# Single PSUM banks, moved sums and a four-buffer weight ring in a hybrid decoder block

## The chip, the cores and the metric

The kernel runs on one core of a Trainium2 chip. The metric is device time in microseconds (us) of one execution, as the median of the runs shown. The engines are TensorE (PE in the profile, its weight loads PEld), VectorE (DVE), ScalarE (ACT), GpSimd (POOL) and SyncE (SP, which issues the DMAs here).

## What is computed

One decoder block over 512 tokens of 1024 channels, all in float32: a mixer (a Mamba-2 scan and a causal pooling, merged by gates), a residual, and an MLP. The change lies where the mixer ends and the MLP begins, and in how the accumulator banks are named everywhere.

```python
h = rmsnorm(x, norm_mix_w) * (1.0 + scale_m) + shift_m
x = x + gate_m * hybrid_mixer(h, w_in, conv_w, ..., w_branch_ssd, pool_w, ..., w_branch_pool, w_out)
h = rmsnorm(x, norm_mlp_w) * (1.0 + scale_f) + shift_f
x = x + gate_f * (jnp.square(jax.nn.relu(h @ w_up)) @ w_down)      # 1024 -> 4096 -> 1024
return rmsnorm(x, norm_final_w)
# shift_*, scale_*, gate_* = split(silu(c) @ w_ada + b_ada): 48 columns of 128
```

## The kernel before, in words

**Layout.** Channels lie on the 128 partitions and the 512 tokens (T) along the free axis; a weight unit gives 128 output channels. Every float32 operand is split into a rounded part `hi` and a rest `lo` (ACT makes `hi`, DVE makes `lo`), and a product is three matmuls, hi·hi, hi·lo and lo·hi (`mm3`, L158 to L162). A unit of 1024 by 128 weights is 8 × 3 = 24 matmuls of 512 columns.

**Order of the work.** The first part (L220 to L299) is an order written out by hand. Everything behind it is handed to a scheduler, which orders the instructions of each engine by their place in the program, with the ones under `tc.high_priority()` first. Within one buffer the users come in program order. An engine then executes its list strictly in order, and the waits between engines follow from who writes and reads which tile.

**Buffers.** `Slots` (L43) is a first-in first-out list of buffers: `get` takes the oldest free one. `RAW` holds weights as they arrive, 4 buffers until the MLP, then 8, of which the last four lie in two large `sz` tiles (L754 to L756). `HL` holds split weights (8, in the MLP 12). `S` has 50 tiles of 512 columns. The `pad` tiles are left over from the pooling; in the MLP `U` (pads 0 and 1) holds the output of an up unit while it is squared and split, `Y4` (pads 5 and 8) a quarter of a pair's weights.

**Accumulators.** PSUM has eight banks of 512 columns. Banks 0 to 3 are single tiles `ps0` to `ps3`. Banks 4 to 7 are the halves of two tiles of two banks, `duo0` (4 and 5) and `duo1` (6 and 7), allotted once (L94 to L100). `PU` serves the weight units, `PS` the scan; from the gates on (L648) `PU` has all eight. The profile calls the tiles `ps` and `duo`.

**The mixer.** Four groups of the scan (`ssd_group`, L419) are woven with the weight units of the next group. `sc`, the scores, keeps one bank of `PS` for the whole group and is read by DVE at L452; `bk` is copied out of a bank by ACT at L429; the transposes (L455) and the output `yd` (L499) take further banks. Then come 8 gate units, 8 pool units (L654 to L658, DVE reads each bank at L656), 8 more gate units and 8 units of `w_out`.

**The modulation.** `ada(j)` (L172) loads 512 KB of `w_ada` into a `RAW` buffer and reduces it on DVE to column j of `mod` (L176). Each call stands behind a unit; the last three (45 to 47) stand behind the two halves of the norm (L742).

**The turn to the MLP.** The last three units of `w_out` run by halves of the tokens (L726), each half followed by the norm (L733) and the modulated row `h2` (hi and lo) with its unsplit source `hf` (8 tiles: six `S`, two `U`). Then `run_jobs` (L869) goes through a list of jobs; before a job runs, the weights of the next one are loaded.

- `up_first` (L937): four up units at once, by halves, in banks `PU`, `PU`, `AC`, `AC` (the free list of `PU` is 2 and 3 from L817, that of `AC` 0 and 1). Behind its matmuls stand, in program order, the shift of `hf` on ACT (L945), the sums `h2t` of `hf` (L947: four DVE operations of 256 columns, two casts and two subtractions for each of four pairs, L768 to L775), one matmul into each `duo` tile (L952), and then `activated` (L919) for the four banks: Relu (L922) into a tile of `U`, Square (L923), cast and subtraction (L765, L766).
- four `up_plain` jobs (L961), one unit each, in a bank of `PU`.
- three times: eight `down_plain` units and four `Pair` jobs (Strassen-like products of 256 columns, two banks of `BE` and one of `AC`, L825 to L863), which need `h2t`. The Relu of a pair reads its two `BE` banks in one instruction of 2 × 256 columns.
- the last down units and the final norm.

Of the kernel before, what the change touches and what calls it, by code (L numbers as in the profile page):

```python
# [7 lines left out]
F32 = mybir.dt.float32  # L8
F32R = mybir.dt.float32r
AF = mybir.ActivationFunctionType  # L10
ALU = mybir.AluOpType

P = 128
T = 512
# [24 lines left out]
OTHER = (0, 1, 4, 5, 8)  # L39
H = T // 2  # L40
# [21 lines left out]
def block_kernel(tc, xT, crow, arow, par, adaT, wstart, wz, wx, wpool_in, wgate, wpw, wbs, wbp, wout, wup, wdn, out):  # L62
# [3 lines left out]
    with (  # L66
# [6 lines left out]
        def slots(name, n, shape=(P, T), where=sb, first=0):  # L73
            def make(i, dt):
                count[0] += 1
                i += first
                return where.tile(list(shape), dt, tag=f"{name}{i}", name=f"{name}{i}_{count[0]}", bufs=1)
            return Slots(make, n)
# [3 lines left out]
        def D(i, dt, o=0):  # L82

            count[0] += 1
            w = 1024 if i < NRAW else 1088
            return sb.tile([P, w], dt, tag=f"d{i}", name=f"d{i}_{count[0]}", bufs=1)[:, o:o + 1024]
# [3 lines left out]
        MT = Slots(lambda i, dt: D(NRAW + NHL + i, dt).rearrange("p (h k) -> p h k", h=HG), 3)  # L90
        SM = slots("sm", 4, (P, NC))
        SM.put(*[SM.get() for _ in range(4)])

        duo = [psp.tile([P, 2, T], F32, name=f"duo{i}") for i in range(2)]  # L94

        def bank(i, dt):
            if i >= 4:
                return duo[(i - 4) // 2][:, i % 2, :]
            count[0] += 1
            return psp.tile([P, T], F32, tag=f"ps{i}", name=f"ps{i}_{count[0]}", bufs=1)  # L100

        PU, PS = Slots(bank, 8), Slots(bank, 8)
        PU.free, PS.free = PU.free[:NPU], PS.free[NPU:]

        par_t = sb.tile([P, NPAR], F32, name="par_t")
# [66 lines left out]
        def ada(j, at=RAW):  # L172

            r = at.get()
            sp.dma_start(r, adaT[j])
            dve.tensor_tensor_reduce(r, r, cbc, 1.0, col("b_ada", j), ALU.mult, ALU.add, mod[:, j:j + 1])  # L176
            at.put(r)
# [536 lines left out]
        for j in range(5):  # L714
            ps = unit(wout[j], mg)
            residual(ps, j, 16)
            PU.put(ps)
            ada(40 + j)
        for k in range(8):
            dve.tensor_scalar(  # L720
                amod[:, 8 + k:9 + k], mod[:, 32 + k:33 + k], 1.0, col("nmlp", k), ALU.add, ALU.mult)
        w = [load_unit(wout[j], at=S, cols=T) for j in (5, 6, 7)]
        h2 = [(S.get(F32R), S.get(F32R)) for _ in range(8)]
        U = Slots(lambda i, dt: slots("pad", 1, (P, T + 16), first=OTHER[i]).get(dt)[:, :T], 2)
        hf = [S.get() for _ in range(6)] + [U.get() for _ in range(2)]
        for t0, t1 in HALVES:  # L726
            for j in (5, 6, 7):
                ps = PU.get()
# [10 lines left out]
                dve.scalar_tensor_tensor(lo, t, shift, hi.bitcast(F32), ALU.add, ALU.subtract)  # L739
            PU.put(R)  # L740
        free(mg)
        for j in range(45, 48):  # L742
            ada(j)

# [5 lines left out]
        for p_, t in zip((SZ, SZ), later):  # L752
            p_.put(t)
        raws = [SZ.get(), SZ.get()]  # L754
        RAW = Slots(lambda i, dt: D(i, dt) if i < 4 else
                    raws[i // 2 - 2][:, 2 * (i % 2):2 * (i % 2) + 2, :].rearrange("p a b -> p (a b)"), 8)  # L756
        HL = Slots(lambda i, dt: D(NRAW + i, dt, 48), 12)
        HL0 = Slots(lambda i, dt: D(NRAW + i, dt), 12)
        HL0.free = HL.free
        Y4 = Slots(lambda i, dt: slots("pad", 1, (P, T + 16), first=OTHER[3 + i]).get(dt)[:, :T], 2)  # L760
        Y4S = Slots(lambda i, dt: slots("pad", 1, (P, T + 16), first=APART[i][0]).get(dt)[:, APART[i][1]:APART[i][1] + T], 4)

        def two(src, dst):
# [13 lines left out]
        def moving(plain, ts):  # L777

            cut = lambda t, i: tuple(x[:, i * H:(i + 1) * H] for x in t)
            return {  # L780
                "B11": [cut(plain[2 * m], 0) for m in range(4)],
                "B21": [cut(plain[2 * m + 1], 0) for m in range(4)],
                "B22": [cut(plain[2 * m + 1], 1) for m in range(4)],
                "T1": [cut(ts[m][0], 0) for m in range(4)], "T3": [cut(ts[m][0], 1) for m in range(4)],
                "T4": [cut(ts[m][1], 0) for m in range(4)], "T2": [cut(ts[m][1], 1) for m in range(4)],
            }
# [25 lines left out]
            Y4.put(y4)  # L812
            return {"S1": s1, "A11": a11, "S2": s2, "A12": a12, "S4": s4, "S3": s3, "A22": a22}

        BE = Slots(lambda i, dt: duo[i][:, :, :], 2)
        AC = slots("ps", 2, (P, T), psp)
        PU.free = [2, 3]  # L817

# [6 lines left out]
        class Pair:  # L825
            def __init__(self, w, b, done):
                self.w, self.b, self.done = w, b, done
# [3 lines left out]

            def open(self):
                self.be, self.s5 = BE.get(), U5.get()
                self.c11, self.c12 = self.be[:, 0, :H], self.be[:, 1, :H]
                product(self.c12, self.a["S1"], self.b["T1"], True)
                with tc.high_priority():
                    act.copy(self.s5, self.c12)
# [18 lines left out]

            def close(self):
                product(self.c12, self.a["S4"], self.b["B22"])
                self.done(0, self.be[:, :, :H], 1)
                BE.put(self.be)  # L860
                product(self.ac[:, :H], self.a["A22"], self.b["T4"])
                self.done(1, self.ac.rearrange("p (a b) -> p a b", a=2), -1)
                AC.put(self.ac)  # L863

        s5_t = slots("pad", 1, (P, T + 16), first=OTHER[2]).get()[:, :T]
        U5 = Slots(lambda i, dt: s5_t[:, i * H:(i + 1) * H], 2)
        ab = lambda t: t.rearrange("p (a b) -> p a b", a=2)

        def run_jobs(jobs):  # L869

            last = None
            jobs[0].prepare()
            for n, job in enumerate(jobs):
                after = jobs[n + 1] if n + 1 < len(jobs) else None
                if isinstance(job, Pair):
                    if n == 0 or not isinstance(jobs[n - 1], Pair):
                        job.open()
                    job.first()
                    if last:
                        last.close()  # L880
                    if after:
                        after.prepare()
                    job.middle()
                    if isinstance(after, Pair):
                        after.open()
                    job.third()
                    last = job
                else:
                    if last:
                        last.close()  # L890
                    last = None
                    if after:
                        after.prepare()
                    job.run()

        def load_plain(src, i, at=None, cols=1024):

# [14 lines left out]
            RAW.put(r)  # L912
            return [parts[4 * (k % 2) + k // 2] for k in range(8)]

        h2t = [[(S.get(F32R), S.get(F32R)) for _ in range(2)] for _ in range(4)]
        us = []
        hb = moving(h2, h2t)

        def activated(q, p, i, ps, sign):  # L919

            u = U.get()
            act.activation(ab(u), ps, AF.Relu, scale=float(sign))  # L922
            act.activation(u, u, AF.Square)  # L923
            two(u, us[2 * p + i])
            U.put(u)

        class Plain:
            def __init__(self, load, run):
                self.load, self.body = load, run

# [5 lines left out]

        def up_first(w):  # L937

            ps = [PU.get(), PU.get(), AC.get(), AC.get()]
            for t0, t1 in HALVES:  # L940
                for k in range(8):
                    for i in range(4):
                        mm3(ps[i][:, t0:t1], w[i][k], h2[k], k == 0, k == 7, t0, t1)
            for k in range(8):
                act.activation(hf[k], hf[k], AF.Identity, bias=mod[:, 24 + k:25 + k])  # L945
            for m in range(4):
                sums(*hf[2 * m:2 * m + 2], *h2t[m])  # L947
            S.put(*hf[:6])
            U.put(*hf[6:])
            us.extend((S.get(F32R), S.get(F32R)) for _ in range(8))  # L950
            for b in duo:
                pe.matmul(b[:, 0, :], h2[0][0][:, :P], h2[0][0], start=True, stop=True)  # L952
            for i in range(4):
                activated(0, i // 2, i % 2, ab(ps[i]), 1)
            PU.put(*ps[:2])
            AC.put(*ps[2:])

        def up(q, p):
            return Pair(wup[4 * q + p], hb, lambda i, ps, sign: activated(q, p, i, ps, sign))

        def up_plain(p, i):  # L961

            def f(w):
                ps = PU.get()
                for k in range(8):
                    mm3(ps, w[k], h2[k], k == 0, k == 7)
                activated(0, p, i, ab(ps), 1)
                PU.put(ps)
            return Plain(lambda: load_plain(wup[p], i), f)

# [49 lines left out]
                PU.put(R)  # L1020

        jobs = [Plain(lambda: [load_plain(wup[i // 2], i % 2, HL) for i in range(4)], up_first)] + [up_plain(p, i) for p in (2, 3) for i in range(2)]
        for q in range(3):
            jobs += [down_plain(q, (0, 1))] + [down_plain(q, (j,)) for j in range(2, 8)] + [up(q + 1, p) for p in range(4)]
        jobs += [down_plain(3, (0, 1))] + [down_plain(3, (j,)) for j in (2, 3, 4)]
# [80 lines left out]
```

## Time and profile before

| | |
|---|---|
| median of 3 runs | 1003.28 us (1002.08 to 1005.58) |
| the profiled execution | 1003.27 us |
| its span, first to last instruction | 1001.6 us |
| mean granted TensorE clock | 0.992 |
| busy in the span | PE 970.7, DVE 668.3, ACT 522.5, POOL 62.5 us |
| DMA | 129.62 MB, mean 129 GB/s |

1.67 us of the profiled execution lie outside its span. PE is busy for all but 30.9 us of it, so the table of waits, restricted to PE, is the shortest way to what could be saved: its rows say which instruction of PE stood idle, and the last event it had waited for. A row "PE ps L160 <- ACT pad L922: 6.8, 1, 6.8" reads: matmuls of line 160 into tiles `ps` waited for an ACT instruction of line 922, 6.8 us in total, in 1 wait, the longest of 6.8 us. In the timeline a row is start, duration, engine, line, operation, out<-in, shape, count, and in brackets the idle time just before. Matmuls overlap, so the rate of PE is the distance from start to start, not the duration.

### The profile page before, as it was taken

Reading aid. Unit: us, or ns where it says so; the run is one execution under the profiler, and the core shown is the slowest. Engines: PE = TensorE matmul, PEld = TensorE weight load, DVE = VectorE, ACT = ScalarE, POOL = GpSimd, SP = SyncE. Lnnn points to the kernel's source line nnn. Section 1 sums busy time; section 2 is a strip of 40 time slices with the busy share of each in tenths; the row PEclk is TensorE's granted clock in tenths of the full one; section 3 lists DMA queues with packets and bytes.
Section 4 is the critical chain, followed back from the end, with each engine's and each line's share of the span. In section 5 each row is a group of like instructions: output and inputs, shape, how many; then the busy total and the mean of one; then the engine's idle time right before and its main releaser. Section 6 shows DMA issues by size and latency. Waiting matters only on the chain.

```text
span 1001.6 us, 13351 instructions
## 1 busy us (share of the span) xinstructions
PE 970.7 (97%) x5174; PEld 815.4 (81%) x5174; DVE 668.3 (67%) x969; ACT 522.5 (52%) x805; POOL 62.5 (6%) x71
## 2 busy tenths in 40 slices
PE   8998999999999999999999999979999999999997
PEld 6877787887878878777878888968899889889986
DVE  6995959467766886888774565675557646755533
ACT  5497997677438733463312342574236326524732
POOL 0101220120102022200000000000000000000000
PEclk9999999999999999999999999989999999999998
DMA  9746343433353234437875444331224125213102
GB/s 349 288 129 190 104 130 105 108 125 101 100 147 106 85 100 121 137 125 251 274 244 167 155 158 130 102 98 53 64 96 158 53 74 170 70 56 132 38 1 84
DMA packets 62913, 129.62 MB, mean 129 GB/s; under 512 B 4801, under 2 KB 29505, under 8 KB 62850
## 3 DMA queue, kind: packets, MB, share of 16 engines
q1 hardware_dynamic: 62850, 128.77, 40.1%
q8 instruction: 40, 0.66, 0.3%
q14 instruction: 23, 0.19, 0.1%
HBM read 126.53 MB, written 2.23 MB: 129 GB/s over the span
## 4 chain that ended last, share of the span: by engine, by line
PE 57%; DVE 6%; DMA 5%; issue 4%; ACT 2%; POOL 1%; POOLq 0%; DVEq 0%; ACTq 0%
PE ps L160 12%; PE ps L161 12%; PE ps L162 12%; PE ps L823 7%; PE duo L823 5%; DMA d<-adaT 3%; PE duo L160 2%; PE duo L161 2%; PE duo L162 2%; DVE d L176 1%; POOL pad L567 1%; PE duo L499 1%; DVE d L766 0%; PE duo L483 0%; ACT d L150 0%
## 5 line engine op out<-in xcount | busy, mean ns | idle before, releaser
L160 PE MATMUL ps<-s,d 128*128 128x512 f32 (+1 forms) x930 | 360.8, 389 | 9.8 <-ACT pad L922 6.8
L161 PE MATMUL ps<-s,d 128*128 128x512 f32 (+1 forms) x930 | 354.9, 382 | 0.9 <-DVE s L131 0.8
L162 PE MATMUL ps<-s,d 128*128 128x512 f32 (+1 forms) x930 | 354.5, 381 | 0.0
L160 PEld LDWEIGHTS ps<-s,d 128*128 128x128 f32 x930 | 175.0, 188 | 48.9 <-ACT pad L922 7.5
L161 PEld LDWEIGHTS ps<-s,d 128*128 128x128 f32 x930 | 175.3, 188 | 35.4 <-issue 1.8
L162 PEld LDWEIGHTS ps<-s,d 128*128 128x128 f32 x930 | 175.0, 188 | 34.2 <-issue 0.6
L150 ACT CAST d<-d 128x1024 fp32r<-128x1024 f32 x89 | 92.8, 1044 | 111.7 <-PE ps L161 56.1
L151 DVE TENSOR_TENSOR d<-d,d 128x1024 fp32r<-128x1024 f32 x89 | 110.9, 1247 | 55.5 <-ACT d L150 50.5
L765 ACT CAST d<-d 128x1024 fp32r<-128x1024 f32 x40 | 41.7, 1049 | 86.1 <-PE ps L161 60.7
L765 ACT CAST d<-sz 128x1024 fp32r<-128x1024 f32 x36 | 37.6, 1050 | 74.3 <-PE ps L161 54.5
L994 DVE SCALAR_TENSOR_TENSOR xs<-ps,mod,xs 128x512 f32<-128x512 f32 x29 | 21.5, 751 | 69.3 <-PE ps L162 69.3
L766 DVE TENSOR_TENSOR d<-d,d 128x1024 fp32r<-128x1024 f32 x40 | 48.7, 1224 | 23.2 <-ACT d L765 21.5
L766 DVE TENSOR_TENSOR d<-sz,d 128x1024 fp32r<-128x1024 f32 x36 | 43.9, 1224 | 28.1 <-ACT d L765 25.1
L160 PE MATMUL duo<-s,d 128*128 128x512 f32 (+1 forms) x158 | 59.4, 378 | 2.8 <-DVE xs L656 2.4
L161 PE MATMUL duo<-s,d 128*128 128x512 f32 (+1 forms) x158 | 58.8, 372 | 0.0
L162 PE MATMUL duo<-s,d 128*128 128x512 f32 (+1 forms) x158 | 58.6, 372 | 0.0
L823 PE MATMUL duo<-s,d 128*128 128x256 f32 x432 | 58.1, 282 | 0.0
L823 PE MATMUL ps<-s,d 128*128 128x256 f32 x432 | 55.9, 280 | 0.1
L823 PEld LDWEIGHTS duo<-s,d 128*128 128x128 f32 x432 | 53.7, 188 | 2.6 <-DVE duo L848 1.5
L823 PEld LDWEIGHTS ps<-s,d 128*128 128x128 f32 x432 | 53.0, 188 | 0.7 <-ACT duo L843 0.7
L176 DVE CUSTOM_DVE_ANT_0 d<-d,d,par_t 128x1024 f32<-128x1024 f32 x32 | 40.8, 1278 | 16.9 <-DMA d<-adaT 16.7
L451 ACT ACTIVATE d<-d,ncs 128x128 f32<-128x128 f32 x128 | 41.3, 391 | 10.7 <-POOL d L447 10.5
(268 smaller groups left out, 1263.3 us busy)
## 6 DMA issues: line engine op xcount, KB each, us to landing
d<-adaT SPq DMA_DIRECT2D x32, 512.0 KB, 4.3
d<-wx SPq DMA_DIRECT2D x18, 512.0 KB, 3.6
d<-wz SPq DMA_DIRECT2D x16, 512.0 KB, 3.4
d<-cs_d SPq DMA_DIRECT2D x16, 512.0 KB, 5.8
d<-wbs SPq DMA_DIRECT2D x16, 512.0 KB, 3.4
d<-wgate SPq DMA_DIRECT2D x16, 512.0 KB, 3.9
d<-wdn SPq DMA_DIRECT2D x16, 512.0 KB, 3.9
sz<-wdn SPq DMA_DIRECT2D x16, 512.0 KB, 3.9
```

Of the source, the lines that this page charges most:

```text
L150: act.copy(hi[:, :w], r[:, a:a + w])
L151: (low or dve).tensor_tensor(lo[:, :w], r[:, a:a + w], hi[:, :w].bitcast(F32), ALU.subtract)
L160: pe.matmul(ps, whi, xhi[:, t0:t1], start=start, stop=False)
L161: pe.matmul(ps, whi, xlo[:, t0:t1], start=False, stop=False)
L162: pe.matmul(ps, wlo, xhi[:, t0:t1], start=False, stop=stop)
L176: dve.tensor_tensor_reduce(r, r, cbc, 1.0, col("b_ada", j), ALU.mult, ALU.add, mod[:, j:j + 1])
L451: act.activation(m[:, i, :], m[:, i, :], AF.Exp, bias=ncs[:, c, g * HG + i:g * HG + i + 1])
L499: pe.matmul(yd[o:o + 64, i * P:(i + 1) * P], xdt[:, i * P + o:i * P + o + 64], m[:, 2 * i + hh, :], start=True, stop=True)
L765: act.copy(dst[0], src)
L766: dve.tensor_tensor(dst[1], src, dst[0].bitcast(F32), ALU.subtract)
L823: pe.matmul(ps, x, y, start=start and m == 0 and i == 0, stop=m == 3 and i == 2, skip_group_check=True)
L994: dve.scalar_tensor_tensor(x1[j], ps[i], mod[:, 40 + j:41 + j], x1[j], ALU.mult, ALU.add)
```

## The change

All eight banks become single tiles `ps0` to `ps7`; the two `BE` banks of a pair are two of them, and the Relu of a pair's first output is two instructions of 256 columns. `up_first` takes the two `AC` banks and the second banks of the two `BE` pairs in place of `PU`'s, so `PU`'s two banks stay free for the plain units. `hf`'s last two tiles are `Y4`'s in place of `U`'s. The shift and the sums of `hf` become a function that stands behind the fourth plain up unit. `RAW` has four buffers until then and eight from there on. `ada(45)` to `ada(47)` stand behind the units 2, 3 and 4 of `w_out`.

```diff
-        duo = [psp.tile([P, 2, T], F32, name=f"duo{i}") for i in range(2)]
-        def bank(i, dt):
-            if i >= 4:
-                return duo[(i - 4) // 2][:, i % 2, :]
...
-        PU, PS = Slots(bank, 8), Slots(bank, 8)
+        PU, PS = slots("ps", 8, (P, T), psp), slots("ps", 8, (P, T), psp)
...
             ada(40 + j)
+            if j > 1:
+                ada(43 + j)
...
-        U = Slots(lambda i, dt: slots("pad", 1, (P, T + 16), first=OTHER[i]).get(dt)[:, :T], 2)
-        hf = [S.get() for _ in range(6)] + [U.get() for _ in range(2)]
+        Y4 = Slots(lambda i, dt: slots("pad", 1, (P, T + 16), first=OTHER[3 + i]).get(dt)[:, :T], 2)
+        hf = [S.get() for _ in range(6)] + [Y4.get() for _ in range(2)]
...
-        for j in range(45, 48):
-            ada(j)
...
+        RAW.free = RAW.free[:4]
...
-        BE = Slots(lambda i, dt: duo[i][:, :, :], 2)
+        banks = [slots("ps", 1, (P, T), psp, first=4 + i).get() for i in range(4)]
+        BE = Slots(lambda i, dt: (banks[2 * i], banks[2 * i + 1]), 2)
...
-                self.done(0, self.be[:, :, :H], 1)
+                self.done(0, (self.c11, self.c12), 1)
...
                     job.run()
+                    if job.after:
+                        job.after()
...
-            act.activation(ab(u), ps, AF.Relu, scale=float(sign))
+            n = T // len(ps)
+            for i_, part in enumerate(ps):
+                act.activation(u[:, n * i_:n * (i_ + 1)], part, AF.Relu, scale=float(sign))
...
         def up_first(w):
-            ps = [PU.get(), PU.get(), AC.get(), AC.get()]
+            ps = [AC.get(), AC.get(), banks[1], banks[3]]
...
-            for k in range(8):
-                act.activation(hf[k], hf[k], AF.Identity, bias=mod[:, 24 + k:25 + k])
-            for m in range(4):
-                sums(*hf[2 * m:2 * m + 2], *h2t[m])
-            S.put(*hf[:6])
-            U.put(*hf[6:])
             us.extend((S.get(F32R), S.get(F32R)) for _ in range(8))
-            for b in duo:
-                pe.matmul(b[:, 0, :], h2[0][0][:, :P], h2[0][0], start=True, stop=True)
+            for b in banks[::2]:
+                pe.matmul(b, h2[0][0][:, :P], h2[0][0], start=True, stop=True)
...
+        def h2_sums():
+            for m in range(4):
+                for k in (2 * m, 2 * m + 1):
+                    act.activation(hf[k], hf[k], AF.Identity, bias=mod[:, 24 + k:25 + k])
+                h2t.append([(S.get(F32R), S.get(F32R)) for _ in range(2)])
+                sums(*hf[2 * m:2 * m + 2], *h2t[m])
+                if m < 3:
+                    S.put(*hf[2 * m:2 * m + 2])
+            Y4.put(*hf[6:])
+            RAW.free += range(4, 8)
+            hb.update(moving(h2, h2t))
...
+        jobs[-1].after = h2_sums      # jobs: up_first and the four up_plain
```

More of the change, by code (lines that the diff above doesn't have):

```diff
@@ L92, in block_kernel @@
         SM.put(*[SM.get() for _ in range(4)])
-        duo = [psp.tile([P, 2, T], F32, name=f"duo{i}") for i in range(2)]
-        def bank(i, dt):
-            if i >= 4:
-                return duo[(i - 4) // 2][:, i % 2, :]
-            count[0] += 1
-            return psp.tile([P, T], F32, tag=f"ps{i}", name=f"ps{i}_{count[0]}", bufs=1)
-        PU, PS = Slots(bank, 8), Slots(bank, 8)
+        PU, PS = slots("ps", 8, (P, T), psp), slots("ps", 8, (P, T), psp)
         PU.free, PS.free = PU.free[:NPU], PS.free[NPU:]
@@ L759, in block_kernel @@
         HL0.free = HL.free
-        Y4 = Slots(lambda i, dt: slots("pad", 1, (P, T + 16), first=OTHER[3 + i]).get(dt)[:, :T], 2)
+        U = Slots(lambda i, dt: slots("pad", 1, (P, T + 16), first=OTHER[i]).get(dt)[:, :T], 2)
         Y4S = Slots(lambda i, dt: slots("pad", 1, (P, T + 16), first=APART[i][0]).get(dt)[:, APART[i][1]:APART[i][1] + T], 4)
@@ L833, in open @@
                 self.be, self.s5 = BE.get(), U5.get()
-                self.c11, self.c12 = self.be[:, 0, :H], self.be[:, 1, :H]
+                self.c11, self.c12 = self.be[0][:, :H], self.be[1][:, :H]
                 product(self.c12, self.a["S1"], self.b["T1"], True)
@@ L858, in close @@
                 product(self.c12, self.a["S4"], self.b["B22"])
-                self.done(0, self.be[:, :, :H], 1)
+                self.done(0, (self.c11, self.c12), 1)
                 BE.put(self.be)
                 product(self.ac[:, :H], self.a["A22"], self.b["T4"])
-                self.done(1, self.ac.rearrange("p (a b) -> p a b", a=2), -1)
+                self.done(1, (self.ac,), -1)
                 AC.put(self.ac)
@@ L866, in block_kernel @@
         U5 = Slots(lambda i, dt: s5_t[:, i * H:(i + 1) * H], 2)
-        ab = lambda t: t.rearrange("p (a b) -> p a b", a=2)
         def run_jobs(jobs):
@@ L913, in load_plain @@
             return [parts[4 * (k % 2) + k // 2] for k in range(8)]
-        h2t = [[(S.get(F32R), S.get(F32R)) for _ in range(2)] for _ in range(4)]
-        us = []
-        hb = moving(h2, h2t)
+        us, h2t, hb = [], [], {}
         def activated(q, p, i, ps, sign):
             u = U.get()
-            act.activation(ab(u), ps, AF.Relu, scale=float(sign))
+            n = T // len(ps)
+            for i_, part in enumerate(ps):
+                act.activation(u[:, n * i_:n * (i_ + 1)], part, AF.Relu, scale=float(sign))
             act.activation(u, u, AF.Square)
@@ L927, in block_kernel @@
         class Plain:
+            after = None
             def __init__(self, load, run):
@@ L943, in up_first @@
                         mm3(ps[i][:, t0:t1], w[i][k], h2[k], k == 0, k == 7, t0, t1)
-            for k in range(8):
-                act.activation(hf[k], hf[k], AF.Identity, bias=mod[:, 24 + k:25 + k])
-            for m in range(4):
-                sums(*hf[2 * m:2 * m + 2], *h2t[m])
-            S.put(*hf[:6])
-            U.put(*hf[6:])
             us.extend((S.get(F32R), S.get(F32R)) for _ in range(8))
-            for b in duo:
-                pe.matmul(b[:, 0, :], h2[0][0][:, :P], h2[0][0], start=True, stop=True)
+            for b in banks[::2]:
+                pe.matmul(b, h2[0][0][:, :P], h2[0][0], start=True, stop=True)
             for i in range(4):
-                activated(0, i // 2, i % 2, ab(ps[i]), 1)
-            PU.put(*ps[:2])
-            AC.put(*ps[2:])
+                activated(0, i // 2, i % 2, (ps[i],), 1)
+            AC.put(*ps[:2])
         def up(q, p):
             return Pair(wup[4 * q + p], hb, lambda i, ps, sign: activated(q, p, i, ps, sign))
+        def h2_sums():
[9 more added lines that the diff above has]
+            hb.update(moving(h2, h2t))
         def up_plain(p, i):
@@ L966, in f @@
                     mm3(ps, w[k], h2[k], k == 0, k == 7)
-                activated(0, p, i, ab(ps), 1)
+                activated(0, p, i, (ps,), 1)
                 PU.put(ps)
```

## The prediction

> **What bounds the kernel now.** I read the page's first part, then the waits of PE alone, then the timelines around the longest waits.
>
> ```profile
> span 1001.6 us, 13351 instructions
> PE 970.7 (97%) x5174; PEld 815.4 (81%) x5174; DVE 668.3 (67%) x969; ACT 522.5 (52%) x805; POOL 62.5 (6%) x71
> ```
>
> ```profile
> PE ps L160 <- ACT pad L922: 6.8, 1, 6.8
> PE duo L499 <- DVE d L452: 2.7, 1, 2.7
> PE duo L160 <- DVE xs L656: 2.4, 1, 2.4
> ...
> PE duo L455 <- ACT s L429: 1.4, 1, 1.4
> ...
> PE duo L160 <- DVE xs L693: 1.0, 2, 0.6
> ```
>
> PE is the bound: 30.9 us of the span are not PE work, and the change can bring little beyond those. The largest wait stands between `up_first` and the first plain up unit (PE, then ACT and DVE):
>
> ```profile
> 660.39 0.64 PE L952 MATMUL duo<-s 128*128 128x512 f32 x2
> 667.82 0.79 PE L160 MATMUL ps<-s,d 128*128 128x512 f32 x1 [6.79 <-ACT pad L922]
> ...
> 672.22 0.39 PE L161 MATMUL ps<-s,d 128*128 128x512 f32 x1
> 672.46 0.39 PE L162 MATMUL ps<-s,d 128*128 128x512 f32 x1
> ```
>
> ```profile
> 659.41 1.05 ACT L765 CAST d<-sz 128x1024 fp32r<-128x1024 f32 x1 [0.83 <-PE ps L161]
> ...
> 662.25 1.04 ACT L765 CAST d<-d 128x1024 fp32r<-128x1024 f32 x1
> ...
> 666.62 0.62 ACT L765 CAST s<-pad 128x512 fp32r<-128x512 f32 x1 [2.29 <-DVE pad L773]
> 667.16 0.60 ACT L922 ACTIVATE pad<-ps 128x512 f32<-128x512 f32 x1
> ```
>
> The plain unit needs a bank of `PU`, and both are `up_first`'s until a Relu (L922) has read them. That Relu writes a `U` tile, and both `U` tiles hold the last two `hf` until the last sums (L773) and their cast are through. So PE stands for the sums. Then it starts slowly: from 667.82 to 672.22 ten matmuls start 0.44 us apart, behind it 0.24.
>
> The second wait is of another kind:
>
> ```profile
> 510.61 0.50 PE L160 MATMUL duo<-s,d 128*128 128x512 f32 x1 [2.37 <-DVE xs L656]
> ...
> 511.65 0.52 PE L161 MATMUL duo<-s,d 128*128 128x512 f32 x1
> ...
> 515.28 0.39 PE L161 MATMUL duo<-s,d 128*128 128x512 f32 x1
> 515.51 0.39 PE L162 MATMUL duo<-s,d 128*128 128x512 f32 x1
> ```
>
> ```profile
> 509.87 0.68 DVE L656 TENSOR_TENSOR xs<-xs,duo 128x512 f32<-128x512 f32 x1
> ```
>
> I followed the free lists by hand: the pool units go to the banks 0, 4, 5, 6, 7, 3, 2, 1, and at 510.61 unit 2 begins, in bank 5. DVE is reading unit 1, in bank 4: the other half of the same tile. With eight banks in turn, nothing in bank 5 is awaited; the tile is what makes PE wait. The same lists put `bk` and the first transposes of group 2 into 7 and 6 (L455 <- L429), `sc` and `yd` of group 0 into 5 and 4 (L499 <- L452), and units 3 and 4 of `w_out` into 6 and 7 (one L160 <- L693). Four waits on partner banks.
>
> **Part by part, against the profiled execution, 1003.27 us** (1.67 outside its span; the median, 1003.28, agrees).
>
> *`up_first` and `U`.* `PU`'s banks 2 and 3 are free, so the first plain unit starts when `up_first` ends at 661.03. Its weights are no hindrance, see below. Gone are 6.79 us of idle time and the slow start: 4.40 us for ten matmuls that take 2.4 at the later distance (0.24), so 2.0. Together 8.8.
>
> What is late next: the third plain unit takes bank 2 again, at 661.03 + 2 × 24 × 0.23 = 672.1, and needs the Relu of the first. ACT ends its four casts at 663.3; four Relus, Squares and casts (0.60 + 0.62, the Square taken as the cast, + 0.62) make 7.4, then one Relu: 671.3. That is 0.8 us in time.
>
> *Sums moved.* The work is the same, later. From the rows below, on ACT it is 8 shifts of 0.71 and 8 casts of 0.62, 10.6 us.
>
> ```profile
> L945 ACT ACTIVATE s<-s,mod 128x512 f32<-128x512 f32 x6 | 4.0, 712 | 0.0
> L765 ACT CAST s<-pad 128x512 fp32r<-128x512 f32 x34 | 21.0, 617 | 2.8 <-DVE pad L773 2.3
> L922 ACT ACTIVATE pad<-duo 128x512 f32<-128x512 f32 x12 | 7.1, 592 | 0.0
> L837 ACT COPY pad<-duo 128x256 f32<-128x256 f32 x12 | 4.4, 368 | 7.5 <-PE duo L823 7.5
> ```
>
> ```profile
> 661.00:673.00 12.00, 5.21 (x15) 4.11 (x15) 8.43 (x12) 9.62 (x17) 0.00 (x0) 0.72 0.49 153
> 673.00:735.00 62.00, 61.83 (x273) 50.69 (x272) 33.13 (x40) 19.36 (x25) 0.00 (x0) 1.00 0.18 52
> 735.00:1001.00 266.00, 258.86 (x1689) 234.77 (x1687) 148.19 (x191) 120.33 (x185) 0.00 (x0) 0.99 0.27 87
> ```
>
> In the windows (PE, PEld, DVE, ACT) ACT is idle for 42 and DVE for 29 of the 62 us before the first pair, which needs the sums. I cost the move at nothing; that slack is the cover, and without it each microsecond past the first pair's start would be one lost.
>
> *Single banks.* The pool unit: 2.37 us idle, and a slow start from 511.65 to 515.28: nine matmuls in 3.63 in place of 9 × 0.23 = 2.1, so 1.5. Together 3.9. Bank 7 for unit 4 of `w_out`: one of the two L693 waits, at least 1.0 − 0.6 = 0.4. The scan's two waits, 2.7 + 1.4 = 4.1, need a choice. There the scheduler orders the whole stage anew once the waits are gone, and which wait comes next no row shows. The upper end is 4.1; the lower end a loss as large as the longest of these waits, −2.7. I take half the gain, 2.0, nearer to the gain since PE is asked for nothing new.
>
> The row of the clock bears on two of these terms: after idle times of 6.79 and of 2.37 us matmuls started 0.44 and 0.40 us apart for some 4 us. [...]
>
> *Relu in two.* 12 pairs, each 2 × 0.37 (a copy of 256 columns, L837) in place of 0.59 on ACT: 1.8 us in a stretch where ACT is busy 120.3 of 266. Nothing; if ACT were the bound there, 1.8. [...]
>
> *`RAW`, `ada`, `Y4`.* Rows of SP's waits, of the page's DMA part and of its groups:
>
> ```profile
> SPq L799 <- DVE d L802: 20.7, 2, 13.7
> SPq L902 <- PE ps L183: 14.6, 1, 14.6
> d<-wdn SPq DMA_DIRECT2D x16, 512.0 KB, 3.9
> d<-adaT SPq DMA_DIRECT2D x32, 512.0 KB, 4.3
> L176 DVE CUSTOM_DVE_ANT_0 d<-d,d,par_t 128x1024 f32<-128x1024 f32 x32 | 40.8, 1278 | 16.9 <-DMA d<-adaT 16.7
> L766 DVE TENSOR_TENSOR d<-sz,d 128x1024 fp32r<-128x1024 f32 x36 | 43.9, 1224 | 28.1 <-ACT d L765 25.1
> ```
>
> Before, plain units' weights lay in `sz` tiles and SP stood 14.6 us until the norm's sums (L183) had left them; in the first four buffers they can come as soon as `up_first`'s are split. Three `ada` issues move ahead of the last loads of `w_out` on SP, and each holds a buffer for 4.3 + 1.3 us; the four buffers share them, so the last loads come some 6 us later at worst, about one unit (24 × 0.23 = 5.5 us). None of PE's longer waits above stands for a load of `w_out`, so I take the lead to be more than a unit and cost this at nothing; without that lead it is 6 us. `Y4` is freed later, and a pair's quarter (L799) waits on SP for it: SP stood 13.7 us at that line before without a wait of PE behind it. Nothing, with a rival for it.
>
> Sum: 8.8 + 3.9 + 0.4 + 2.0 = 15.1, so **988.2 us**.
>
> **Rivals.**
> 1. *Only the MLP's stall goes.* The new order puts other waits in place of the partner waits; the DVE list that stands for `w_ada`'s DMAs is still there. 1003.27 − 8.8 − 0.4 = 994.1. For it: the 2.0 rest on an order that is made anew. Against: unit 2's wait has its cause in the tile.
> 2. *The wait moves to the third plain unit.* If ACT's list has rests of the sums ahead of the Relus, the 0.8 us of margin is gone: half of the 10.6 us ahead costs 4.5, all of it 9.8. Taking the half: 992.7. For it: before, just these casts stood ahead of the Relu. Against: they now come later in the program.
> 3. *Slower: SP stands at the pair's quarter.* Its place in SP's list is fixed before the run; if the sums end late, every load of down weights behind it waits. Four buffers cover four plain and four down units: 661 + 8 × 5.5 = 705, less 3.9 for the load and some 2.3 for the split: from 699 on each microsecond is lost, from 714 on the kernel is slower than before. Sums that follow the fourth plain unit (683) and take all their 10.6 us end at 694, close to it. Ending at 720 it would be 988.2 + 21 = 1009.2.
> 4. *It doesn't do what it says*: the waits have another cause than tile and `U`; about 1003.
>
> **Chances.** Forecast 0.62, rival 1 0.18, rival 2 0.11, rival 3 0.05, rival 4 0.04. A measurement of this kernel can tell about 0.3%, 3 us, from no change. Forecast and rivals 1 and 2 are faster by more: 0.91, rounded down to 0.90; rival 4 and mixtures are the same, 0.06; rival 3 slower, 0.04. The range begins 3 us below the whole 4.1 of the scan (986.1), for waits of PE that I did not assign (30.9 us are not PE work): 983.1. It ends with rival 1 and the scan's loss, 994.1 + 2.7 = 996.8. It holds the forecast and nearly all of rivals 1 and 2.
>
> **What would show it.** In the waits of PE the row L160 <- L922 is gone, and so are those of L455 on L429, L499 on L452 and L160 on L656; the start of the first plain unit follows L952 at once. If rival 2 holds, L160 <- L922 stays with a shorter time, two units later; if rival 3, SP's row for L799 grows past 25 us and L160 waits for L766 on DVE or L765 on ACT among the down units. A new wait of over 2 us in the scan would make the fourth term wrong, and PE idle for 7 us or more before the first pair the whole forecast.

## The result and the profile after

The changed kernel takes 979.72 us (median of 4 runs, 978.66 to 979.87) where the kernel before, run beside it, takes 1004.42 (4 runs, 1002.08 to 1005.58): a ratio of 0.9755, interval 0.9733 to 0.9777. It is faster, as forecast, but by 23.5 us between the two profiled executions in place of 15.1, and 979.7 lies below the range given.

The head of the page of after, and the waits of PE (engine, tile and line <- what was waited for: us in total, times, the longest):

```profile
span 978.1 us, 13339 instructions
PE 958.0 (98%) x5174; PEld 810.9 (83%) x5174; DVE 669.1 (68%) x969; ACT 522.7 (53%) x817; POOL 63.1 (6%) x71
```

```profile
PE ps L174 <- DVE s L230: 5.2, 1, 5.2
PE ps L151 <- ACT pad L549: 1.5, 1, 1.5
...
PE ps L151 <- ACT s L121: 1.1, 1, 1.1
...
PE ps L523 <- POOL s L514: 0.9, 1, 0.9
```

The same work now has lower line numbers, by 9 up to the MLP (L160 is L151, L183 is L174, L656 is L647), and L922 is L916. All four rows that the prediction meant to remove are gone: L160 <- L922 (6.8), L499 <- L452 (2.7), L160 <- L656 (2.4), L455 <- L429 (1.4). New are L121 with 1.1 and L523 with 0.9. L174 <- L230, near the start, is no work of the change: it was 2.2 before, and 2.2 to 5.2 in the runs below.

PE stands for 20.1 us of the span where it stood for 30.9. That is 10.8 of the 23.5 us gained; the busy time fell by 12.7 though the same 5174 matmuls ran, since matmuls that start late (0.50 us long at 523.25 before) or run slowly (0.63 at 512.39) count as busy for longer than the usual 0.39 us. In the second pair of profiles (e11 and e12 below) it is 14.1 and 8.8 of 22.9 us; the split hangs in part on L174's wait, which is 3.0 us longer in the profile of after than in that of before. So between a good third and a good half of the gain was in no row of waits. The timeline of PE after, at the turn to the MLP:

```profile
648.05 0.28 PE L153 MATMUL ps<-s,d 128*128 128x256 f32 x1
648.17 0.63 PE L942 MATMUL ps<-s 128*128 128x512 f32 x2
648.63 0.40 PE L151 MATMUL ps<-s,d 128*128 128x512 f32 x1
648.87 0.39 PE L152 MATMUL ps<-s,d 128*128 128x512 f32 x1
```

The first plain unit follows the two single matmuls at once and at 0.23 us from start to start. To see where the rest came from, five rows cut the run into stages; their starts, before and after:

```profile
70.19 0.57 ACT L429 COPY s<-duo 128x512 f32<-128x512 f32 x1
...
425.69 0.58 ACT L558 COPY pad<-ps 128x512 f32<-128x512 f32 x1
...
545.04 0.68 DVE L656 TENSOR_TENSOR sz<-sz,ps 128x512 f32<-128x512 f32 x1
...
642.47 0.17 DVE L196 RECIPROCAL sm<-sm 128x2 f32<-128x2 f32 x1 [0.99 <-ACT sm L195]
...
702.28 1.43 DVE L994 SCALAR_TENSOR_TENSOR xs<-ps,mod,xs 128x512 f32<-128x512 f32 x2 [4.85 <-PE ps L162]
```

```profile
70.72 0.57 ACT L420 COPY s<-ps 128x512 f32<-128x512 f32 x1
...
420.58 0.58 ACT L549 COPY pad<-ps 128x512 f32<-128x512 f32 x1
...
533.69 0.69 DVE L647 TENSOR_TENSOR sz<-sz,ps 128x512 f32<-128x512 f32 x1 [0.69 <-PE ps L153]
...
629.49 0.17 DVE L187 RECIPROCAL sm<-sm 128x2 f32<-128x2 f32 x1 [1.04 <-ACT sm L186]
...
680.94 1.43 DVE L996 SCALAR_TENSOR_TENSOR xs<-ps,mod,xs 128x512 f32<-128x512 f32 x2 [4.85 <-PE ps L153]
```

They are the first copy of `bk`, the last copy of the pooling's input, the multiplication of the last pool unit, the second norm's reciprocal (of its second half) and the first update by a down unit. Both kernels were profiled a second time (e11 and e12 below), and the table gives the length of each stage in both profiles of each:

| stage | before, e11 | after, e12 | gain of the means | predicted |
|---|---|---|---|---|
| start to the first `bk` | 70.2, 70.2 | 70.7, 70.5 | −0.4 | 0 |
| the scan | 355.5, 354.6 | 349.9, 350.1 | 5.1 | 2.0 |
| gates and pool units | 119.4, 120.1 | 113.1, 113.1 | 6.6 | 3.9 |
| gates, `w_out`, norm | 97.4, 97.3 | 95.8, 95.1 | 1.9 | 0.4 |
| the turn, to the first down unit | 59.8, 59.6 | 51.4, 51.5 | 8.2 | 8.8 |
| three stages of pairs, end | 299.3, 298.5 | 297.1, 297.1 | 1.8 | 0 |

The marks are events of ACT and DVE, and PE's list shifts against them: the turn holds 292 matmuls before and 301 after, the stage of `w_out` 512 and 506. So I also summed, by stage, what the distances from start to start of PE's matmuls exceed the usual one (the median behind a matmul of the same shape). In the turn this falls from 10.4 and 10.1 to 0.4 and 0.4 us, in `w_out` from 3.3 and 3.2 to 2.8 and 2.1: of the gain in the row of `w_out`, 1 us or so belongs to the turn.

The terms that were worked out for the turn hold. What exceeds the forecast, some 8 us, lies outside the turn.

### The profile page after: what moved, and what is told of

Same layout as the page of the kernel before. It is cut to its first block, busy times and chain, and to the rows that moved or that the text cites. A ratio compares the mean times of both kernels' runs of the same rounds, so it can differ in the third digit from the quotient of the medians.

```text
span 978.1 us, 13339 instructions
## 1 busy us (share of the span) xinstructions
PE 958.0 (98%) x5174; PEld 810.9 (83%) x5174; DVE 669.1 (68%) x969; ACT 522.7 (53%) x817; POOL 63.1 (6%) x71
## 4 chain that ended last, share of the span: by engine, by line
PE 85%; ACT 4%; DVE 3%; DMA 3%; issue 2%; POOL 1%; SPq 0%; DVEq 0%; POOLq 0%; ACTq 0%
PE ps L151 22%; PE ps L152 21%; PE ps L153 21%; PE ps L816 12%; PE ps L287 4%; PE ps L490 1%; DMA d<-cs_d 1%; ACT d L141 1%; DMA d<-adaT 1%; DVE d L142 1%; PE ps L474 1%; ACT d L442 1%; ACT L357 1%; PE ps L470 1%; ACT L442 1%
## 5 line engine op out<-in xcount | busy, mean ns | idle before, releaser
L151 PE MATMUL ps<-s,d 128*128 128x512 f32 (+1 forms) x1088 | 416.8, 384 | 3.7 <-ACT pad L549 1.5
L152 PE MATMUL ps<-s,d 128*128 128x512 f32 (+1 forms) x1088 | 411.6, 378 | 0.0
L153 PE MATMUL ps<-s,d 128*128 128x512 f32 (+1 forms) x1088 | 411.3, 378 | 0.0
L151 PEld LDWEIGHTS ps<-s,d 128*128 128x128 f32 x1088 | 204.1, 188 | 47.6 <-issue 2.8
L153 PEld LDWEIGHTS ps<-s,d 128*128 128x128 f32 x1088 | 204.3, 188 | 38.4
L152 PEld LDWEIGHTS ps<-s,d 128*128 128x128 f32 x1088 | 204.3, 188 | 38.2 <-issue 1.1
L142 DVE TENSOR_TENSOR d<-d,d 128x1024 fp32r<-128x1024 f32 x89 | 111.2, 1250 | 49.6 <-ACT d L141 49.5
L816 PE MATMUL ps<-s,d 128*128 128x256 f32 x864 | 104.4, 280 | 0.1
L816 PEld LDWEIGHTS ps<-s,d 128*128 128x128 f32 x864 | 102.9, 188 | 1.0 <-ACT ps L836 0.7
L757 ACT CAST d<-sz 128x1024 fp32r<-128x1024 f32 x32 | 33.4, 1050 | 71.1 <-PE ps L152 50.1
L758 DVE TENSOR_TENSOR d<-d,d 128x1024 fp32r<-128x1024 f32 x44 | 53.4, 1224 | 21.9 <-ACT d L757 20.3
L758 DVE TENSOR_TENSOR d<-sz,d 128x1024 fp32r<-128x1024 f32 x32 | 39.0, 1224 | 19.8 <-ACT d L757 18.6
L353 DVE SCALAR_TENSOR_TENSOR s<-ps,par_t,s 128x511 f32<-128x511 f32 (+2 forms) x54 | 40.1, 743 | 2.4 <-ACT s L351 2.0
L287 PE MATMUL ps<-s,d 128*128 128x512 f32 x144 | 35.5, 397 | 0.5 <-ACT s L275 0.5
L287 PEld LDWEIGHTS ps<-s,d 128*128 128x128 f32 x144 | 26.3, 188 | 8.2 <-ACT s L275 2.9
L758 DVE TENSOR_TENSOR s<-pad,s 128x512 fp32r<-128x512 f32 x34 | 23.2, 688 | 8.0 <-ACT s L757 7.7
L438 POOL TENSOR_SCALAR_AFFINE_SELECT d<-d 128x1024 f32<-128x1024 f32 x16 | 19.9, 1241 | 123.4 <-ACT cd L435 62.4
```

The lines of the kernel that those rows point to most:

```text
L142: (low or dve).tensor_tensor(lo[:, :w], r[:, a:a + w], hi[:, :w].bitcast(F32), ALU.subtract)
L151: pe.matmul(ps, whi, xhi[:, t0:t1], start=start, stop=False)
L152: pe.matmul(ps, whi, xlo[:, t0:t1], start=False, stop=False)
L153: pe.matmul(ps, wlo, xhi[:, t0:t1], start=False, stop=stop)
L287: pe.matmul(first[u], w[u][i // 2], h[k][i % 2], start=k == 0 and i == 0, stop=k == 7 and i == 2)
L353: dve.scalar_tensor_tensor(t[:, sh:], ps[:, :T - sh], w(3 - sh), t[:, sh:], ALU.mult, ALU.add)
```

## The experiments

Theory: the gain has two separate causes, the tile of two banks (everything outside the turn) and the banks of `up_first` (the turn). Rivals: the turn's other edits (`U`, the sums, `RAW`, `ada`) carry a part; the split Relu does; or banks under the partner's name moved something else. A ratio is always to the kernel before, run beside the kernel in question.

**e1, the single banks alone**, in the kernel before (with the Relu in two, which the separate tiles need):

```diff
-        duo = [psp.tile([P, 2, T], F32, name=f"duo{i}") for i in range(2)]
...
-        PU, PS = Slots(bank, 8), Slots(bank, 8)
+        PU, PS = slots("ps", 8, (P, T), psp), slots("ps", 8, (P, T), psp)
...
-        BE = Slots(lambda i, dt: duo[i][:, :, :], 2)
+        banks = [slots("ps", 1, (P, T), psp, first=4 + i).get() for i in range(4)]
+        BE = Slots(lambda i, dt: (banks[2 * i], banks[2 * i + 1]), 2)
```

> The kernel before with eight single banks and the pair's Relu in two, nothing else of the change. Theory (a tile of two banks makes PE wait for the reader of the partner bank, in every stage): all that lies outside the turn to the MLP goes, by the two traces some 5 us in the scan, 1 up to the pool units, 5 there, 2 in w_out and the norm, 2 in the pairs, so about 989 to 990 us, while the wait L160 <- L922 of 6.8 us stays. Rival (the gains outside the turn come from the moved w_ada columns, the weight ring or the split Relu, which shift the order): only the waits that were counted in the prediction go, 997 us or more.

Measured: 985.08 us (984.88 to 986.54), ratio 0.9809, interval 0.9783 to 0.9835. That is more than any theory had: 18.4 us between the profiled executions. Stages: scan 350.0, pool 114.3, `w_out` and norm 93.4, turn 57.8, pairs 297.2. In sum all the gain outside the turn is here, 16.1 us against the mean of before (the pool stage lacks 1.2 of it, `w_out` has 2 more). In the waits of PE the turn's own row stays, with 4.0 in place of 6.8:

```profile
PE ps L152 <- ACT pad L917: 4.0, 1, 4.0
```

**e2, the turn's edits alone**, the changed kernel with the `duo` tiles back (the edit above the other way round; the Relus stay in two).

> The changed kernel, but with the banks 4 to 7 in two tiles of two banks as before. Theory: the turn alone, 8.3 us by the traces, so about 996 us; the waits L499 on L452, L455 on L429 and L160 on L656 are as before, and each pair starts some 0.2 us late as before. Rival: 990 us or less, if the moved w_ada columns or the ring bring the rest.

Measured: 996.7 us (993.87 to 1000.4), ratio 0.9924, interval 0.9898 to 0.995, as the theory said. The partner waits are back, one of them larger than before:

```profile
PE duo L159 <- DVE xs L655: 3.1, 1, 3.1
PE duo L159 <- DVE xs L692: 2.4, 2, 1.8
PE duo L498 <- DVE d L451: 2.3, 1, 2.3
```

The turn gains 10.0 (49.8 us), and 4.6 of them are lost again in `w_out` and the norm (101.9), where one of the waits is a unit's 1.8 us for its partner bank. With the tiles of two banks each edit of the order moves the partner waits about. The stages of pairs take 298.8, as in the kernel before, though the Relu is split: they gain by the tiles, not by the Relu.

**e3, the same two tiles with other partners** (4 with 6, 5 with 7), in the kernel before:

```diff
-                return duo[(i - 4) // 2][:, i % 2, :]
+                return duo[i % 2][:, (i - 4) // 2, :]
```

> The kernel before with one line changed: banks 4 and 6 share a tile, and 5 and 7, so that banks used one after the other lie in different tiles. Theory: the wait of L160 on L656 at the second pool unit goes with its slow start (some 4 to 5 us), the turn's 6.8 us stays, the pairs keep their 0.2 us, and in the scan some waits go and others come: 998 to 1001 us. Rival (the wait at the pool unit is DVE's list behind the DMAs of w_ada, not the tile): it stays, and the time is within 0.3% of before.

Measured: 1002.62 us (999.97 to 1003.59), ratio 0.9973, interval 0.9958 to 0.9988: hardly faster. The wait of the pool units shrinks to 0.7, but the scan gets new waits:

```profile
PE duo L532 <- POOL s L523: 4.4, 1, 4.4
...
PE duo L434 <- ACT s L429: 1.4, 1, 1.4
...
PE duo L160 <- DVE xs L656: 0.7, 1, 0.7
```

The pool stage takes 115.9 us (3.9 less than the mean of before), the scan 360.4 (5.3 more). L434 <- L429 is a new partner wait: by the free lists `bk` of the last group lies in bank 5 and `sc` in bank 7, which share a tile here, and L434 reads nothing that L429 writes. The larger one, L532 <- L523, is not: L523 writes `ssum`, the operand of L532, which comes late in the new order of the scan; why, was not traced. Nothing but the partners differs between the two kernels, so the pool unit's wait that shrinks and L434's that comes are those of partner banks. Shown, then: PE waits for a reader of the other half of its tile.

**e4, the Relu in two alone**, in the kernel before.

> The kernel before with the Relu of a pair's two banks in two instructions, nothing else. Theory (the pairs' 2 us come from the tiles): no change, within 0.3%; a pair still shows the extra 0.2 us of PE. Rival (the split itself frees the first bank earlier): the pairs become 2 us shorter in all, 1002 us.

Measured: 1004.98 us (1001.33 to 1007.78), ratio 1.0002, interval 0.9986 to 1.0018. Nothing, as predicted for this part.

**e5, `ada(45)` to `ada(47)` back behind the norm**, in the changed kernel.

```diff
-            if j > 1:
-                ada(43 + j)
...
+        for j in range(45, 48):
+            ada(j)
```

> The changed kernel with the last three w_ada columns behind the norm again. Theory (the moved columns bring nothing to the turn and stand in DVE's list among the last units of w_out): what the single banks alone had more up to the second norm, 1.3 us, comes back: 978 to 979 us, the turn as in the changed kernel. Rival (their early end frees the buffer that the plain units' weights need): the plain units start late, 982 us or more.

Measured: 978.59 us (977.75 to 979.0), ratio 0.9741, interval 0.9717 to 0.9766. The row L151 <- ACT s L121 is gone and the stage of `w_out` takes 93.5; the turn takes 52.2, 0.8 more than after. It is the fastest kernel of the study, by an amount that the intervals do not part from after.

**e6, `RAW` with its eight buffers from the start**, in the changed kernel (both lines on `RAW.free` left out).

> The changed kernel with eight weight buffers from the start of the MLP. Theory (the first plain unit's weights come at the norm's sums as before, some 15 us ahead of their use): no change, 979 to 980.5 us. Rival (they come too late now that no wait covers them): a wait for a cast or a subtraction at the first plain unit, 982 us or more.

Measured: 981.98 us (980.04 to 982.74), ratio 0.9772, interval 0.9749 to 0.9795. I had expected nothing. The third plain unit waits; the timelines of PE, DVE and ACT in e6:

```profile
657.83 0.39 PE L153 MATMUL ps<-s,d 128*128 128x512 f32 x1
660.04 0.50 PE L151 MATMUL ps<-s,d 128*128 128x512 f32 x1 [1.83 <-ACT pad L915]
...
660.92 0.63 PE L151 MATMUL ps<-s,d 128*128 128x512 f32 x1
...
663.90 0.52 PE L152 MATMUL ps<-s,d 128*128 128x512 f32 x1
```

```profile
658.01 0.69 DVE L792 TENSOR_TENSOR d<-d 128x512 f32<-128x512 f32 x1 [2.24 <-DMA d<-wup]
658.62 1.89 DVE L757 TENSOR_TENSOR s<-pad,s 128x512 fp32r<-128x512 f32 x3
```

```profile
659.40 0.60 ACT L915 ACTIVATE pad<-ps 128x512 f32<-128x512 f32 x1 [1.32 <-DVE s L757]
```

With eight buffers the first addition of a pair's weights (L792) stands in DVE's list ahead of the subtractions of the up units, and DVE waits 2.24 us for its DMA. The subtractions would free a tile of `U`, the Relu (L915) waits for that tile, and PE for the bank of the Relu. In the changed kernel the same addition starts at 656.42 and waits for nothing. So the four buffers are worth some 2 us; the intervals of e6 and after overlap, and what parts them is this wait and the slow start behind it (the turn takes 55.2, 3.8 more than after).

**e7, the sums ahead of the Relus in the program**, in the changed kernel: `h2_sums()` is called in `up_first`, not behind the fourth plain unit.

> The changed kernel with the sums of the modulated rows ahead of the up units' Relus in program order again; the free banks and the tiles of hf stay as changed. Theory (the free banks let the first two plain units start; the Relu of the first is behind the sums on ACT, which is 2 us or so later than the third unit wants its bank): the wait moves to the third plain unit, 1 to 4 us, so 981 to 984 us. Rival (the place of the sums is what matters, not the banks): the wait of 4 us and more of the single banks alone is back at the first plain unit, 985 us.

Measured: 980.23 us (979.17 to 980.74), ratio 0.9758, interval 0.9733 to 0.9782. The same time, below the range expected; the third plain unit now waits for the first one's Relu, but only 0.9 us.

**e8, `up_first` in the banks of before**, in the changed kernel:

```diff
-            ps = [AC.get(), AC.get(), banks[1], banks[3]]
+            ps = [PU.get(), PU.get(), AC.get(), AC.get()]
```

> The changed kernel with up_first in the two banks of the plain units again; the sums stay behind the plain units. Theory (the Relu follows the four casts on ACT at once): the first plain unit waits some 3 us for the first Relu, without or with a slow start of 1.5 us, so 982.5 to 985 us. Rival (the place of the sums alone does it): 980 us.

Measured: 983.53 us (981.68 to 984.82), ratio 0.9791, interval 0.9765 to 0.9816. The first plain unit waits again, and some six matmuls behind it are slow, 0.43 us from start to start in place of 0.23:

```profile
PE ps L151 <- ACT pad L916: 2.8, 1, 2.8
```

**e9, e1 with `up_first` in other banks** and none of the turn's other edits: the line of e8 the other way round, in e1.

> The kernel of e1 (single banks, Relu in two) with one thing more: the first four up units in the banks of AC, 5 and 7, so that PU's banks 2 and 3 are free behind them. The last two modulated rows still lie in the U tiles, the sums still stand ahead of the Relus in the program, RAW has its eight buffers from the start, ada 45 to 47 stand behind the norm. Theory A (the turn is a matter of banks alone: the first plain unit waits for a bank, and the Relus are not so late that the third unit waits long): the 4.0 us on L917 and the slow start behind it go, PE's next wait is the third plain unit's for bank 2, 11.1 us after the first unit's start (about 659), against the first plain unit's Relu, which in e1 started at 660.1 behind four Relus: 0 to 1.5 us. 979.5 to 982. Theory B (the freed U tiles or the place of the sums carry a part): the third unit waits 2 to 4 us with a slow start, 982.5 to 985.

Measured: 980.84 us (980.07 to 983.39), ratio 0.9767, interval 0.975 to 0.9783, beside e12, the changed kernel itself, at 0.9748, interval 0.9734 to 0.9762. The 4.0 us of e1 are gone, and what is late next is the third plain unit. PE in e9:

```profile
659.68 0.50 PE L152 MATMUL ps<-s,d 128*128 128x512 f32 x1 [1.63 <-ACT pad L917]
```

The wait is 0.1 us above the upper end of what theory A expected, and the time lies in its range. The banks alone, `up_first`'s among them, bring all but some 2 us, and the two intervals overlap. DVE waits here too for a pair's weights, 0.77 us.

**e10, e5 and e7 together**: the changed kernel with `ada` behind the norm and the sums first.

> The changed kernel with both moves taken back that seemed to bring nothing: ada 45 to 47 behind the norm (e5) and the sums ahead of the Relus (e7). Theory A (neither matters): within 0.3% of e5 and of the changed kernel, 977.5 to 981. Rival (each uses the slack that the other left: ACT has the sums' casts and DVE the three products of ada between the norm and the third plain unit): the third plain unit waits 1 to 3 us for its bank, 980.5 to 984.

Measured: 979.71 us (978.64 to 981.2), ratio 0.9752, interval 0.9737 to 0.9767. The third unit waits 1.7 us, as the rival said; the stage of `w_out` is shorter by about as much, so the time does not move.

**e11 and e12, both kernels once more.**

> The kernel before, once more with a profile: how far its partner waits vary from run to run. If the pool unit's 2.4 us and the scan's 2.7 and 1.4 are fixed by the program, the rows return within 0.3 us. If they hang on when DMAs land, they move by a microsecond or more, and so does the time (1000 to 1008 so far).

> The changed kernel, once more with a profile, on the same chip as e9 and e10: 978.5 to 980. Its time should vary less than that of the kernel before, since no matmul waits for a partner bank any more; the 1.1 us of the first unit of w_out for ACT should return if it is the ada products that hold ACT and DVE there, and not if it was chance.

Measured: 1001.88 us for the one run of e11; 979.05 us for e12 (978.37 to 980.36), ratio 0.9748, interval 0.9734 to 0.9762. The waits of PE in e11:

```profile
PE duo L160 <- DVE xs L656: 3.0, 1, 3.0
...
PE duo L499 <- DVE d L452: 1.8, 1, 1.8
PE duo L455 <- ACT s L429: 1.2, 1, 1.2
```

The partner waits are there in every run of the old tiles, but not of one size: 1.8 to 2.7 us for L499, 2.4 to 3.9 for L656 (3.9 in e4). (e3, with other partners, has other waits.) In e12 L121 shows 0.5 where after had 1.1. With single banks, the five profiles with the moved `ada` have this wait at the start of `w_out` (0.5 to 1.2: after, e6, e7, e8, e12), and e1, e5, e9 and e10, which leave `ada` behind the norm, do not. So the moved `ada` brings it there; e2, with the moved `ada` and the old tiles, does not show it.

## Why the prediction was wrong: the partner banks were worth more than twice what it took

Direction, mechanism and the largest term were right. The step that failed is the size of *Single banks*. It went by PE's idle rows ("30.9 us of the span are not PE work, and the change can bring little beyond those") and halved the scan's: 3.9 + 0.4 + 2.0 = 6.3 us, where the stages outside the turn gained 15.0 by the table, and 16.1 in e1, which has the single banks alone; 8.8 to 12.7 us of the whole gain came out of PE's busy time. Point by point:

- **The turn, 8.8.** Measured 8.2 by the marks, some 10 by PE's distances, of which the stall and its slow start are 9.1. Row gone, slow start gone, the first plain unit behind the single matmuls at once. By the marks, the single banks alone bring 1.9 of the 8.2 (e1, 59.7 to 57.8), the banks of `up_first` 4.4 more (e9, to 53.4; e8, with the banks of before, stands at 56.0), and the other edits together the last 2.0.
- **The scan, 2.0: the largest miss.** "I take half the gain, 2.0, nearer to the gain": it was 5.1, more than the 4.1 called the upper end. The fear of a new order was a guess without a row; with single banks the only wait that came is one of 0.9 us (1.1 in e12). PE's idle time in the stage fell by 3.0 (from 6.0 and 5.1 to 2.5 and 2.7). Nor was 4.1 an upper end: a wait costs PE some 0.16 us beyond its row (2.53 for the 2.37 of unit 2), since the row counts from the end of the last matmul, 0.39 behind its start, and the next would have started 0.23 behind it. And where a wait goes, small ones go that no row shows: what the distances exceed the usual one, idle time included, fell by 4.4 us (29.6 and 28.6 to 24.6 and 24.9). The rest of the 5.1 was not followed wait by wait.
- **The pool units, 3.9: too small.** Measured 6.6. The wait and its slow start were rightly sized. Missing were partner waits with no idle time. Timelines of PE and DVE before, two units later:

```profile
522.31 0.39 PE L160 MATMUL ps<-s,d 128*128 128x512 f32 x1
522.54 0.39 PE L161 MATMUL ps<-s,d 128*128 128x512 f32 x1
522.76 0.39 PE L162 MATMUL ps<-s,d 128*128 128x512 f32 x1
522.99 0.39 PE L160 MATMUL ps<-s,d 128*128 128x512 f32 x1
523.25 0.50 PE L160 MATMUL duo<-s,d 128*128 128x512 f32 x1
523.59 0.39 PE L161 MATMUL duo<-s,d 128*128 128x512 f32 x1
```

```profile
522.51 0.69 DVE L656 TENSOR_TENSOR xs<-xs,duo 128x512 f32<-128x512 f32 x1 [1.50 <-PE duo L162]
```

  L160 follows on L160: PE has done four matmuls of a unit in a `ps` bank and leaves it for unit 4, in bank 7, which starts when DVE ends its read of unit 3, in bank 6 (522.51 + 0.69 = 523.20). By this order the scheduler seems to have foreseen the wait and put matmuls of another unit into it. What is left are starts 0.26 and 0.34 us apart in place of 0.23, 0.15 us lost with no bracket. In the gates and pool units the order L160, L161, L162 is broken at 14 places before and in e2, which has the old tiles, at 4 after, in e1, and in e3, where the neighbours are others. Summed over all matmuls of the stage, what start-to-start distances exceed the usual ones falls from 7.1 and 8.0 (e11) to 0.9 us. The 6.2 of the first pair: 2.5 at unit 2, 1.7 its slow start, 0.8 such switches (0.1 is left after), 1.1 a matmul that waited for DVE (the 0.8 us row L161 <- L131), the rest in single hundredths. That last wait is not one of the tiles: e1 and e9, with single banks, keep 0.6 and 0.8 of it, and e2, with the old tiles, is without it; which edit of the turn takes it away was not found.
- **Pairs, 0.** Measured 1.8, in the same way: before, PE lost 3.6 us in 30 late starts of pair matmuls, after 1.4 in 12. e2 (tiles of two banks, Relu split) loses 3.6, e1 1.3: the tiles again. That the split Relu costs nothing was right (e4).
- **`w_out`, 0.4.** Measured 1.9 by the marks and 0.8 by PE's distances; e1 gained 3.9 and 2.2 here, both L693 waits being gone. The three `ada` that the change puts into this stage take 1 to 2 us of it back (95.8 and 95.1 with them, 93.5 and 93.6 in e5 and e10 without), and give some of that at the turn. I had costed them at nothing, and in sum they are: e5 and after cannot be told apart.
- **`RAW` at nothing.** Its sum was right only because of the edit: undoing it costs some 2 us (e6). I had looked at SP's queue and at the weights of the plain units; the wait is DVE's, for a pair's weights, and what is queued behind that addition is what frees `U`.
- **Rival 1** (only the turn) fell. **Rival 2** (the third plain unit) missed by little: the margin worked out was 0.8 us, the changed kernel shows no wait there, and 0.4, 0.9, 1.6, 1.7 and 1.8 us appear when one edit or more is undone (e5, e7, e9, e10, e6). **Rival 3** did not come: SP waits for `Y4` until the sums have left it, and no matmul waits behind it. The row of SP's queue after:

```profile
SPq L791 <- DVE s L758: 17.1, 2, 16.7
```

  Before, the longest wait at this line was 13.7.

What stays open: for the pairs, which of their late starts stands for which reader was not followed one by one; that they are bound to the tile is shown by e1 and e2. By which step `ada` in `w_out` brings the wait on L121 was not traced, and neither was the part of the scan's gain beyond PE's distances.

## What to carry to other kernels

Under this scheduler a tile over two accumulator banks makes one dependency of two: a matmul into one bank waits for the reader of the other (2.37 us at the pool unit before, a row that e1 does not have). Look at the free lists for banks that are used in turn, and count such a wait at more than its row in the waits: add the matmuls that follow at the slow rate (1.7 us behind those 2.37), and look for places where the matmuls' order breaks off and the start-to-start distance is above the usual one, because there the scheduler may have filled a wait that doesn't show as idle time. Where the next wait is under a microsecond away, as at the third plain unit, each edit that seems free may be what keeps it away; undo them one at a time before calling them useless.

## What the runs showed of the hardware

Behind some of its pauses PE ran at about half its pace. In the kernel before, after the pool unit's pause of 2.37 us, matmuls of 512 columns start 0.43 us apart from 512.39 to 514.96, in place of 0.227 (522.31 to 522.99). The granted clock was 0.50 in this stretch. In the rows below a stretch is followed by its length and PE's busy time, and the third number from the end is the granted clock. The pool unit before, then the turn behind its pause of 6.79 us:

```profile
508.34:511.75 3.41, 1.14 (x5) 0.96 (x6) 3.21 (x6) 0.00 (x0) 0.00 (x0) 1.00 0.78 235
511.75:515.17 3.42, 3.42 (x10) 2.64 (x9) 2.02 (x3) 0.00 (x0) 0.00 (x0) 0.50 0.90 270
```

```profile
665.36:672.19 6.83, 4.38 (x10) 3.47 (x11) 3.85 (x7) 5.48 (x11) 0.00 (x0) 0.50 0.59 186
672.19:676.00 3.81, 3.81 (x18) 3.10 (x17) 1.39 (x2) 2.29 (x5) 0.00 (x0) 1.00 0.00 0
```

In these runs the length of the pause alone does not tell whether the slow matmuls come. Behind the scan, matmuls kept their 0.23 us after pauses of 1.63 us (e9) and 1.66 us (e10); slow ones followed pauses of 1.83 us (e6), 2.37 (before), 2.83 (e8), 3.00 (e11), 4.01 (e1) and 6.79 (before). So e6 loses another 1.6 us by a wait only 0.2 longer than that of e9: the nine distances from 660.62 to 664.26 take 3.64 us in place of 2.04. In the scan before, the 2.65 us of L499 were followed by no slow matmul: from 97.98 to 99.37 they start 0.23 us apart, and the granted clock was 1.00 from 95.33 to 98.74. What decides between these cases was not shown, since no run changed one pause and nothing else.
